# An MLP down-projection in seven block products: eight of its 22 activations, in seven of eight units of a two-layer trunk

## The chip, the cores and the metric

The kernel is one program on one core of a Trainium2 chip. The metric is the device time of one execution in microseconds (us); the kernel before takes 1237.61 us, the median of three runs (1237.38 to 1237.62). A profile comes from one execution of its own.

The engines named here are TensorE (PE; its weight loads are shown as PEld), VectorE (DVE), ScalarE (ACT), GpSimd (POOL) and SyncE (SP), which here issues the DMA transfers of the weights. Each engine works through its own queue of instructions in order, and waits for others by semaphores.

## What is computed

Two layers of a decoder trunk on 512 tokens of 1024 features, in fp32. Each layer is a token mixer (layer 0 attention and short convolution, layer 1 gated linear attention), an MLP, and a gated embedding; all add to the residual `x`. The change is in the second matrix product of the MLP, with `w_down` of 2816 x 1024:

```python
def _conv_ffn(h, w_up, conv_w, conv_b, w_down):
    u = _causal_depthwise_conv(h @ w_up, conv_w) + conv_b
    gate, up = jnp.split(u, 2, axis=-1)
    return (jax.nn.gelu(gate, approximate=False) * up) @ w_down
...
    x = x + _conv_ffn(_rms_norm(x, ffn_norm[i]), ffn_w_up[i], ffn_conv_w[i], ffn_conv_b[i], ffn_w_down[i])
    x = x + _per_layer_embedding(x, p[i], ple_norm[i], ple_w_gate[i], ple_w_proj[i])
```

## The kernel before

**Layout.** Features lie on the 128 partitions and the 512 tokens along the free axis, so `x` is eight tiles `xT[0..7]` of 128 x 512, and the MLP's 2816 inner features are 22 tiles, the activations f = 0 to 21 (`acts`). A product for eight output features' tiles m = 0 to 7 takes weights of 128 x 128 as the stationary operand and an activation tile as the moving one, and adds up in a PSUM bank of 128 x 512.

**Precision.** Each fp32 operand is cut into a high part of reduced precision (`F32R`) and a low part, the remainder. ScalarE copies the high part, VectorE subtracts it from the source for the low one. `mm3` (L158 to L160) then does three matmuls: high x high, high x low, low x high. For weights the cut is in `cut` (L138 high, L139 low): pieces of 1024 columns, from a tile `raw` (two buffers, loaded by SyncE) into `wh` and `wl` (three buffers each). For activations it is `split` (L102, L103; with a gain L105, L106).

**Down-projection.** `project` runs over four units of two output tiles (256 columns of `w_down`). A unit takes the 22 activations in three chunks of eight, eight and six, each with a load and two cuts (halves by columns, `by="b"`); unit 0 begins with the activations 8 to 15, the others with 0 to 7. So a unit is 22 x 2 x 3 = 132 matmuls of 512 columns, and a layer 528. At a unit's end `done` adds both banks to `xT` (L379 in layer 0, L1056 in layer 1) and prepares the tile for the next norm: `advance` in layer 0 splits it with a gain (L105, L106), squares it (L270) and adds the square to `acc` (L271); `blocks` in layer 1 does the like for block forms. Behind the down-projection L324 sums `acc` over the partitions, and the gated embedding follows (`ple1` in layer 1).

**Activations.** `kept` tiles hold the activations in fp32 as the up-projection makes them. `split_acts` cuts f = 0 to 19 for the down-projection, some by pairs (`split_pair`); the last pair, `y`, is cut by `split_pair(NF - 2, y)` just ahead of it.

**Block products.** The up-projection already uses, for the gate columns of units d = 4 to 10, a scheme in which a product of two matrices, each seen as 2 x 2 blocks, needs seven products of blocks instead of eight. The blocks of the weights are (even or odd feature tile) x (left or right 128 columns), those of the activations (even or odd tile) x (left or right 256 tokens). `seven_forms` makes the weights' sums: a plain cut, then four subtractions (L823, L824, L826, L828) in place, and cuts `t13` (L811, L812, wide) and `t2` (narrow); `seven` does the products with 256 columns each (`product`, L846 to L848), on four token-side sums s1 to s4 (`forms`). It adds up in four places, W, V (banks `pa`), X and Y (banks `ps`), with ScalarE copies that seed one from another (L857, L858, L865, L869), and yields between its parts so that other matmuls can be put there. V belongs to both halves of Y; in the up-projection it is copied to SBUF first (`more`, L862).

**Order.** Most of the queues' order is a scheduler's; `manual_schedule` takes the program's order for the engines that it names, `high_priority` puts instructions ahead. In the up-projection the PE order is the program's. The loads stand on SyncE's queue in order of their issue, and each waits for its `raw` buffer.

Of the kernel before, what the change touches and what calls it, by code (L numbers as in the profile page):

```python
# [9 lines left out]
F32 = mybir.dt.float32  # L10
F32R = mybir.dt.float32r
# [3 lines left out]
ALU = mybir.AluOpType  # L15
# [3 lines left out]
P = 128  # L19
S = 512  # L20
D = 1024
NT = S // P
ND = D // P
DFF = 2816
NF = DFF // P
# [3 lines left out]
ET = mybir.EngineType  # L29
# [28 lines left out]
class Kernel:  # L58
# [92 lines left out]

        return get

    def mm3(self, out, lt, rt, start, stop):

        mm = self.nc.tensor.matmul
        (lh, ll), (rh, rl) = lt, rt
        mm(out, lh, rh, start=start, stop=False)  # L158
        mm(out, lh, rl, start=False, stop=False)  # L159
        mm(out, ll, rh, start=False, stop=stop)  # L160

    def rsqrt(self, out, src, scale):

# [631 lines left out]
                out.append((hl[0][:, c], hl[1][:, c]))  # L795
        return out

    def blocks_of(self, raw):

        rv = raw.rearrange("p (j u) n -> p j u n", u=2)  # L800
        return [[rv[:, :, u, c * P : (c + 1) * P] for c in range(2)] for u in range(2)]

    def cut_blocks(self, src, wide=True):

# [9 lines left out]
        n = 2 if wide else 1  # L814
        return lambda j, c: (h[:, n * j + c, :], l[:, n * j + c, :])

    def seven_forms(self, raw):

        nc = self.nc
        (b11, b12), (b21, b22) = self.blocks_of(raw)  # L820
        plain = self.cut_blocks(raw[:, :, :P])

        nc.vector.tensor_tensor(b11, b12, b11, ALU.subtract)  # L823
        nc.vector.tensor_tensor(b12, b22, b12, ALU.subtract)  # L824
        t13 = self.cut_blocks(raw.rearrange("p (j u) n -> p j u n", u=2)[:, :, 0])
        nc.vector.tensor_tensor(b11, b22, b11, ALU.subtract)  # L826
        t2 = self.cut_blocks(b11, False)
        nc.vector.tensor_tensor(b21, b21, b11, ALU.subtract)  # L828
        return plain, t13, t2

    def seven(self, raw, ws, xg, forms):

        nc = self.nc
        H = S // 2
        mm = nc.tensor.matmul
        W, V = self.pa(), self.pa()[:, :H]
        X, Y = self.ps(), self.ps()
        plain, t13, t2 = ws  # L840

        def product(out, w, c, x, first=False):
            kw = dict(skip_group_check=True)
            for j in range(ND // 2):
                (wh, wl), (xh, xl) = w(j, c), x(j)
                mm(out, wh, xh, start=first and j == 0, stop=False, **kw)  # L846
                mm(out, wh, xl, start=False, stop=False, **kw)  # L847
                mm(out, wl, xh, start=False, stop=j == ND // 2 - 1, **kw)  # L848

        def tokens(u, half):  # L850
            c = slice(half * H, (half + 1) * H)
            return lambda j: (xg[2 * j + u][0][:, c], xg[2 * j + u][1][:, c])

        s1, s2, s3, s4 = (lambda j, q=q: forms[j][q] for q in range(4))
        left, right = slice(0, H), slice(H, S)
        product(W[:, left], plain, 0, tokens(0, 0), True)
        nc.scalar.copy(X[:, left], W[:, left])  # L857
        nc.scalar.copy(Y[:, left], W[:, left])  # L858
        yield
        product(V, t13, 0, s1, True)  # L860
        more = self.sp.tile([P, S], F32, tag="acc", name=self.nm("more"), bufs=1)[:, :H]
        nc.scalar.copy(more, V)  # L862
        product(X[:, left], plain, 1, tokens(1, 0))
        product(Y[:, left], t2, 0, s2)
        nc.scalar.copy(X[:, right], Y[:, left])  # L865
        yield
        last = self.cut_blocks(raw.rearrange("p (j u) n -> p j u n", u=2)[:, :, 1])
        product(X[:, right], t13, 1, s3)
        nc.scalar.copy(Y[:, right], X[:, right])  # L869
        yield  # L870
        product(Y[:, left], last, 1, s4)
        product(X[:, right], last, 0, tokens(1, 1))
        yield X, Y, more

    def ffn(self, i, next_gain):
        nc, a, tc = self.nc, self.a, self.tc
        xg, R = self.xg, None
        gain = self.g_ffn[i]
        wu = a["ffn_w_up"][i].rearrange("(k p) n -> p k n", p=P)
        w0, w1, w2, bb = self.fcv  # L880
        with tc.tile_pool(name=f"ffn{i}", bufs=1) as fp:
# [35 lines left out]
            def column(raw, c):  # L917
                return self.cut(raw[:, :, c * P : (c + 1) * P], "b")
# [21 lines left out]
            def split_acts():  # L940
                for f in (8, 10, 12):
                    split_pair(f)
                split_kept(0)
                split_pair(14)
                split_kept(1)
                for f in (16, 18):
                    split_pair(f)

            def gates(d):
                return slice(256 * d, 256 * d + 256)  # L950
# [16 lines left out]
            def prepare(d):  # L967

                rg, rv = loaded(d)
                w1 = column(rv, 1)  # L970
                ws = self.seven_forms(rg)
                return self.seven(rg, ws, xg, forms), w1, column(rv, 0)

            def begin(d, steps, w):

# [6 lines left out]
            first, last = SEVEN  # L982
            scratch = [self.four(fp, F32) for _ in range(ND // 2)]
            late = None
            for d in range(NF // 2):
                g, y = both(), both()
                if first <= d < last:
                    with tc.manual_schedule(engines={ET.PE}):
# [18 lines left out]
                else:  # L1007
# [4 lines left out]
                    todo = []  # L1012
# [21 lines left out]
                u = place(d)  # L1034
                if u is None:
                    u = y
                nc.vector.tensor_tensor(u, g, y, ALU.mult)
                for j in {0: (0, 1), 1: (2, 3)}.get(d, ()):
                    forms.append(self.sums(j, gain, R, scratch[j]))
            split_pair(NF - 2, y)  # L1040
            self.begin_norm(("a0", "a1"))
            done = self.residual(next_gain)
            if i == 1:
                self.forms = []
                halves = []

                def half():
                    if not halves:
                        x = both()
                        halves.extend([x[:, 0], x[:, 1]])  # L1050
                    return halves.pop(0)

                self.half = half

                def done(m, ps):
                    nc.vector.tensor_tensor(self.xT[m], self.xT[m], ps, ALU.add)  # L1056
                    self.blocks(m, next_gain, half)

            self.project(self.rows(a["ffn_w_down"][i]), acts, ND, done, first=(8,))
            if i == 0:  # L1060
                self.end_norm()
            else:
                self.ple1(fp)

    def p_halves(self, i):
        src = self.a["p"][i, 0].rearrange("(t p) e -> p t e", p=P)
# [700 lines left out]
```

## Time and profile before

| | |
|---|---|
| median of three runs | 1237.61 us |
| the profiled execution | 1237.57 us |
| its span, first to last instruction | 1235.8 us |
| instructions | 16256 |
| TensorE matmuls | 6488 |
| DMA, bytes moved | 117.52 MB, mean 95 GB/s |

How to read the profile: a group's row gives line, engine, operation, output <- inputs, their shapes and how often it occurs; then its busy time in us, the mean of one in ns, and the idle time of the engine just before, with what ended it. A timeline's row gives start and duration in us, and in brackets the idle time before it and its releaser. A stretch's row gives its length, and for each engine the busy time with the number of instructions, then the granted clock of TensorE (1.00 is full speed), the busy share of the DMA engines and GB/s. Matmuls overlap in the pipeline, so their starts tell their rate, not their durations.

### The profile page before, as it was taken

How to read it: one execution, taken by the hardware profiler on the slowest of the kernel's cores; microseconds unless marked ns; L12 is line 12 of the kernel's file. 1: busy time of each engine (PE TensorE's matmuls, PEld its weight loads, DVE VectorE, ACT ScalarE, POOL GpSimd, SP SyncE). 2: the span in 40 equal slices, each digit the busy share in tenths (PEclk: the TensorE clock that was granted, in tenths of full speed). 3: DMA queues.
4: the chain of work that ended last, by engine and by line, in shares of the span. 5: the costliest groups of instructions: out<-in, count | busy, mean ns of one | idle time of the engine just before them, and what ended most of it. 6: DMA issues, size and time to landing. Idle time of an engine off the chain costs nothing.

```text
span 1235.8 us, 16256 instructions
## 1 busy us (share of the span) xinstructions
PE 1225.1 (99%) x6488; PEld 1037.8 (84%) x6488; DVE 857.8 (69%) x1337; ACT 611.8 (50%) x975; POOL 44.2 (4%) x64
## 2 busy tenths in 40 slices
PE   9999999999999999999999999999999999999998
PEld 8877788889899888888987888888889989888887
DVE  6886556987778933346679875549977779744495
ACT  7466343555556732234563554435455556533374
POOL 3500000000000000000100000000000000000000
PEclk9999999999999999999999999999999999999999
DMA  7321232323232322222322222332332323322411
GB/s 216 95 79 54 87 103 69 102 69 126 80 112 94 128 94 94 94 85 93 111 91 68 70 68 69 103 99 81 101 109 72 127 79 111 119 94 94 154 42 69
DMA packets 111008, 117.52 MB, mean 95 GB/s; under 512 B 2728, under 2 KB 106210, under 8 KB 110932
## 3 DMA queue, kind: packets, MB, share of 16 engines
q1 hardware_dynamic: 109568, 115.35, 28.4%
q8 instruction: 51, 0.84, 0.3%
q0 software_dynamic: 560, 0.42, 0.3%
q10 hardware_dynamic: 804, 0.70, 0.2%
q14 instruction: 25, 0.20, 0.0%
HBM read 114.37 MB, written 2.10 MB: 94 GB/s over the span
## 4 chain that ended last, share of the span: by engine, by line
PE 88%; DVE 7%; ACT 2%; issue 2%; POOL 1%; DMA 0%; SPq 0%; DVEq 0%; ACTq 0%; POOLq 0%
PE ps L158 18%; PE ps L159 18%; PE ps L160 18%; PE pa L159 5%; PE pa L158 5%; PE pa L160 5%; PE ps L848 3%; PE ps L847 3%; PE ps L846 3%; DVE wl L139 1%; PE pa L848 1%; PE pa L847 1%; PE pa L846 1%; PE ps L1181 1%; PE ps L1179 1%
## 5 line engine op out<-in xcount | busy, mean ns | idle before, releaser
L138 ACT ACTIVATE wh<-raw 128x1024 fp32r<-128x1024 f32 (+4 forms) x184 | 184.3, 1003 | 312.3 <-PE ps L159 258.5
L139 DVE TENSOR_TENSOR wl<-raw,wh 128x1024 fp32r<-128x1024 f32 (+4 forms) x184 | 212.0, 1153 | 166.3 <-ACT wh L138 165.9
L158 PE MATMUL ps<-a,wh 128*128 128x512 f32 x416 | 162.7, 391 | 0.0
L159 PE MATMUL ps<-a,wh 128*128 128x512 f32 x416 | 162.3, 390 | 0.0
L160 PE MATMUL ps<-a,wl 128*128 128x512 f32 x416 | 162.0, 390 | 0.0
L158 PE MATMUL ps<-b,wh 128*128 128x512 f32 x320 | 126.0, 395 | 0.5 <-ACT b L102 0.5
L160 PE MATMUL ps<-b,wl 128*128 128x512 f32 x320 | 125.7, 393 | 0.0
L159 PE MATMUL ps<-b,wh 128*128 128x512 f32 x320 | 125.0, 391 | 0.0
L158 PEld LDWEIGHTS ps<-a,wh 128*128 128x128 f32 x416 | 78.1, 188 | 16.6 <-issue 0.7
L159 PEld LDWEIGHTS ps<-a,wh 128*128 128x128 f32 x416 | 78.2, 188 | 16.3 <-issue 0.3
L160 PEld LDWEIGHTS ps<-a,wl 128*128 128x128 f32 x416 | 78.1, 188 | 16.2
L158 PE MATMUL pa<-a,wh 128*128 128x512 f32 x224 | 87.8, 392 | 0.0
L159 PE MATMUL pa<-a,wh 128*128 128x512 f32 x224 | 87.8, 392 | 0.0
L158 PE MATMUL ps<-four,wh 128*128 128x512 f32 x224 | 87.2, 389 | 0.0
L159 PE MATMUL ps<-four,wh 128*128 128x512 f32 x224 | 87.2, 389 | 0.0
L160 PE MATMUL pa<-a,wl 128*128 128x512 f32 x224 | 87.1, 389 | 0.0
L160 PE MATMUL ps<-four,wl 128*128 128x512 f32 x224 | 87.1, 389 | 0.0
L158 PEld LDWEIGHTS ps<-b,wh 128*128 128x128 f32 x320 | 60.0, 188 | 14.0 <-ACT b L102 1.3
L900 DVE SCALAR_TENSOR_TENSOR zt<-z,vfa,zt 128x511 f32<-128x511 f32 (+1 forms) x92 | 66.9, 744 | 5.9 <-ACT zt L898 5.4
L160 PEld LDWEIGHTS ps<-b,wl 128*128 128x128 f32 x320 | 60.1, 188 | 12.6
L159 PEld LDWEIGHTS ps<-b,wh 128*128 128x128 f32 x320 | 60.1, 188 | 12.4
L811 ACT ACTIVATE wh<-raw 128x1024 fp32r<-128x1024 f32 x42 | 44.4, 1057 | 41.1 <-DVE raw L824 22.1
(423 smaller groups left out, 2620.9 us busy)
## 6 DMA issues: line engine op xcount, KB each, us to landing
raw<-in_ffn_w_up_dram SPq DMA_DIRECT2D x44, 1024.0 KB, 5.0
raw<-in_ffn_w_down_dram SPq DMA_DIRECT2D x16, 1024.0 KB, 4.7
raw<-in_hy_w_in_dram SPq DMA_DIRECT2D x8, 1024.0 KB, 5.1
raw<-in_gla_w_in_dram SPq DMA_DIRECT2D x8, 1024.0 KB, 5.4
raw<-in_ffn_w_down_dram SPq DMA_DIRECT2D x8, 768.0 KB, 4.1
raw<-in_ple_w_gate_dram SPq DMA_DIRECT2D x6, 1024.0 KB, 4.8
raw<-in_gla_w_out_dram SPq DMA_DIRECT2D x4, 1024.0 KB, 4.7
raw<-in_gla_w_in_dram SPq DMA_DIRECT2D x4, 672.0 KB, 4.0
```

Source lines behind the costliest of these rows:

```text
L138: nc.scalar.activation(hv, v, AF.Copy)
L139: nc.vector.tensor_tensor(lv, v, hv.bitcast(F32), ALU.subtract)
L158: mm(out, lh, rh, start=start, stop=False)
L159: mm(out, lh, rl, start=False, stop=False)
L160: mm(out, ll, rh, start=False, stop=stop)
L811: nc.scalar.activation(h, src, AF.Copy)
L846: mm(out, wh, xh, start=first and j == 0, stop=False, **kw)
L847: mm(out, wh, xl, start=False, stop=False, **kw)
L848: mm(out, wl, xh, start=False, stop=j == ND // 2 - 1, **kw)
L900: nc.vector.scalar_tensor_tensor(out=y[:, tap:], in0=z[:, : S - tap], scalar=w[:, f : f + 1], in1=y[:, tap:], op0=ALU.mult, op1=ALU.add,)
L1179: mm(o, lh, rh, start=first and j == 0, stop=False, **kw)
L1181: mm(o, ll, rh, start=False, stop=j == J - 1, **kw)
```

## The change

The 22 rows of activations become A (8 to 13), B (0 to 7) and C (14 to 21). `project` is replaced, for this product alone, by `down`. A unit's C part is done by `seven` in units 0 to 3 of layer 0 and 0 to 2 of layer 1; A and B, and C in unit 3 of layer 1, stay direct. The direct work is a written list `plan` of steps (unit, rows, first and last tile within them, and the unit whose blocks are interleaved, if any), each of three or four tiles and one cut by rows (`by="a"`). In a blocked step, two direct tiles' runs of six matmuls alternate with the parts of `seven`: six direct, W (12), six direct, V with X left and Y left (36), six direct, X right (12), six direct, Y left and X right (24). `pump` counts the three `wh`/`wl` pairs and lets out the next cuts as pairs come free: a cut takes one, a unit's `prepare` two.

V stays in PSUM, and is added from there to both halves of `xT[2s+1]` (L1237); X and Y are added to `xT` as well as the direct banks are (L1170). In layer 0, unit 3 continues its direct sums in X and Y. The C parts of unit 1, and in layer 0 of unit 3, are loaded into the two `zt` tiles, by parity of the row tile, rather than into `raw`. `finish`, which is `advance` or `blocks`, runs for a unit once all blocked steps are done and its sums are complete.

The activations 14 to 21 are cut after the plan's steps 0 to 3 by `split_blocks`, which also makes the token-side sums, two subtractions and additions per half tile, and cuts them into `a0`, `a1`. In the whole program PE has 252 matmuls more: 84 of 256 columns for 48 of 512, seven times. The diff follows, without the three lines in which `mm3` hands on keyword arguments and those in which the up-projection calls the changed functions.

```diff
--- before.py
+++ after.py
@@ -795,10 +795,10 @@
                 out.append((hl[0][:, c], hl[1][:, c]))
         return out
 
-    def blocks_of(self, raw):
+    def by_parity(self, raw):
 
         rv = raw.rearrange("p (j u) n -> p j u n", u=2)
-        return [[rv[:, :, u, c * P : (c + 1) * P] for c in range(2)] for u in range(2)]
+        return rv[:, :, 0], rv[:, :, 1]
 
     def cut_blocks(self, src, wide=True):
 
@@ -814,21 +814,29 @@
         n = 2 if wide else 1
         return lambda j, c: (h[:, n * j + c, :], l[:, n * j + c, :])
 
-    def seven_forms(self, raw):
+    def seven_forms(self, ev, od, raw=None):
 
         nc = self.nc
-        (b11, b12), (b21, b22) = self.blocks_of(raw)
-        plain = self.cut_blocks(raw[:, :, :P])
+        b11, b12, b21, b22 = ev[:, :, :P], ev[:, :, P:], od[:, :, :P], od[:, :, P:]
+        if raw is not None:
+            plain = self.cut_blocks(raw[:, :, :P])
+        else:
+            h, l = (self.wp.tile([P, 1024], F32R, tag=g, name=self.nm(g), bufs=3) for g in ("wh", "wl"))
+            h, l = (x.rearrange("p (j u n) -> p j u n", u=2, n=P) for x in (h, l))
+            for u, b in enumerate((b11, b21)):
+                self.split((h[:, :, u], l[:, :, u]), b)
+            plain = lambda j, c: (h[:, j, c], l[:, j, c])
 
         nc.vector.tensor_tensor(b11, b12, b11, ALU.subtract)
         nc.vector.tensor_tensor(b12, b22, b12, ALU.subtract)
-        t13 = self.cut_blocks(raw.rearrange("p (j u) n -> p j u n", u=2)[:, :, 0])
+        t13 = self.cut_blocks(ev)
         nc.vector.tensor_tensor(b11, b22, b11, ALU.subtract)
         t2 = self.cut_blocks(b11, False)
         nc.vector.tensor_tensor(b21, b21, b11, ALU.subtract)
         return plain, t13, t2
 
-    def seven(self, raw, ws, xg, forms):
+    def seven(self, od, ws, xg, forms, keep=True):
 
 
 
@@ -858,13 +866,15 @@
         nc.scalar.copy(Y[:, left], W[:, left])
         yield
         product(V, t13, 0, s1, True)
-        more = self.sp.tile([P, S], F32, tag="acc", name=self.nm("more"), bufs=1)[:, :H]
-        nc.scalar.copy(more, V)
+        more = V
+        if keep:
+            more = self.sp.tile([P, S], F32, tag="acc", name=self.nm("more"), bufs=1)[:, :H]
+            nc.scalar.copy(more, V)
         product(X[:, left], plain, 1, tokens(1, 0))
         product(Y[:, left], t2, 0, s2)
         nc.scalar.copy(X[:, right], Y[:, left])
         yield
-        last = self.cut_blocks(raw.rearrange("p (j u) n -> p j u n", u=2)[:, :, 1])
+        last = self.cut_blocks(od)
         product(X[:, right], t13, 1, s3)
         nc.scalar.copy(Y[:, right], X[:, right])
         yield
@@ -941,10 +951,28 @@
                 for f in (8, 10, 12):
                     split_pair(f)
                 split_kept(0)
-                split_pair(14)
                 split_kept(1)
-                for f in (16, 18):
-                    split_pair(f)
+            down_forms = []
+            def split_blocks(f, x=None):
+                if x is None:
+                    x = kept[f // 4][:, f % 4 : f % 4 + 2]
+                split_pair(f, x)
+                H = S // 2
+                e, o = x[:, 0], x[:, 1]
+                nc.vector.tensor_tensor(o[:, H:], e[:, H:], o[:, H:], ALU.add)
+                nc.vector.tensor_tensor(e[:, H:], e[:, :H], e[:, H:], ALU.subtract)
+                nc.vector.tensor_tensor(e[:, :H], o[:, H:], e[:, :H], ALU.subtract)
+                nc.vector.tensor_tensor(o[:, :H], o[:, :H], e[:, :H], ALU.subtract)
+                (s2, s3), (s4, s1) = map(split_halves, (e, o))
+                down_forms.append((s1, s2, s3, s4))
+            def split_halves(x):
+                h, l = self.pair(self.fp, "a0", "a1")
+                self.split((h, l), x)
+                return [(h[:, c], l[:, c]) for c in (slice(0, S // 2), slice(S // 2, S))]
 
             def gates(d):
                 return slice(256 * d, 256 * d + 256)
...
@@ -1037,9 +1066,8 @@
                 nc.vector.tensor_tensor(u, g, y, ALU.mult)
                 for j in {0: (0, 1), 1: (2, 3)}.get(d, ()):
                     forms.append(self.sums(j, gain, R, scratch[j]))
-            split_pair(NF - 2, y)
             self.begin_norm(("a0", "a1"))
-            done = self.residual(next_gain)
+            finish = lambda m: self.advance(m, next_gain)
             if i == 1:
                 self.forms = []
                 halves = []
@@ -1051,16 +1079,165 @@
                     return halves.pop(0)
 
                 self.half = half
-
-                def done(m, ps):
-                    nc.vector.tensor_tensor(self.xT[m], self.xT[m], ps, ALU.add)
-                    self.blocks(m, next_gain, half)
-
-            self.project(self.rows(a["ffn_w_down"][i]), acts, ND, done, first=(8,))
+                finish = lambda m: self.blocks(m, next_gain, half)
+            work = [lambda f=f, x=x: split_blocks(f, x) for f, x in ((14, None), (16, None), (18, None), (20, y))]
+            self.down(i, acts, down_forms, both, work, finish)
             if i == 0:
                 self.end_norm()
             else:
                 self.ple1(fp)
+    def down(self, i, acts, forms, both, work, finish):
+        nc, tc = self.nc, self.tc
+        H = S // 2
+        wd = self.a["ffn_w_down"][i].rearrange("(k p) n -> p k n", p=P)
+        rows = {"A": (8, 14), "B": (0, 8), "C": (14, 22)}
+        plan = [(0, "A", 0, 3), (0, "A", 3, 6), (0, "B", 0, 4), (0, "B", 4, 8)]
+        plan += [(1, "A", 0, 3), (1, "A", 3, 6), (1, "B", 0, 4), (1, "B", 4, 8, 0)]
+        plan += [(2, "B", 0, 4, 1), (2, "B", 4, 8, 2)]
+        if i == 0:
+            plan += [(2, "A", 0, 4, 3), (2, "A", 4, 6), (3, "B", 0, 4), (3, "B", 4, 8), (3, "A", 0, 3), (3, "A", 3, 6)]
+            loads = ["A0", "B0", "A1", "B1", "C0", "B2", "C2", "A2", "B3", "A3"]
+            inner = ["C1", "C3"]
+        else:
+            plan += [(2, "A", 0, 3), (2, "A", 3, 6), (3, "B", 0, 4), (3, "B", 4, 8)]
+            plan += [(3, "C", 0, 4), (3, "C", 4, 8), (3, "A", 0, 3), (3, "A", 3, 6)]
+            loads = ["A0", "B0", "A1", "B1", "C0", "B2", "C2", "A2", "B3", "C3", "A3"]
+            inner = ["C1"]
+        blocked = 4 - i
+        plan = [p if len(p) == 5 else p + (None,) for p in plan]
+        got, cuts, gens = {}, {}, {}
+        def cols(u):
+            return slice(2 * P * u, 2 * P * u + 2 * P)
+        def load(key):
+            k0, k1 = rows[key[0]]
+            u = int(key[1])
+            raw = self.raw(k1 - k0, 2 * P)
+            nc.sync.dma_start(raw, wd[:, k0:k1, cols(u)])
+            got[key] = (raw, None)
+        def load_inner(key):
+            k0, k1 = rows[key[0]]
+            u = int(key[1])
+            parts = []
+            for q in range(2):
+                t = both().rearrange("p a (b n) -> p (a b) n", n=2 * P)
+                nc.sync.dma_start(t, wd[:, k0 + q : k1 : 2, cols(u)])
+                parts.append(t)
+            got[key] = (None, parts)
+        def cut(t):
+            u, name, k0, k1, _ = plan[t]
+            cuts[t] = self.cut(got[f"{name}{u}"][0][:, k0:k1], "a")
+            if k1 == rows[name][1] - rows[name][0] and loads:
+                load(loads.pop(0))
+        def prepare(u):
+            raw, parts = got[f"C{u}"]
+            ev, od = parts or self.by_parity(raw)
+            ws = self.seven_forms(ev, od, raw)
+            gens[u] = self.seven(od, ws, acts[14:], forms, False)
+        def cut_done(u):
+            raw, _ = got[f"C{u}"]
+            if raw is not None and loads:
+                load(loads.pop(0))
+            elif raw is None and inner:
+                load_inner(inner.pop(0))
+        todo = []
+        for t, p in enumerate(plan):
+            todo.append((1, lambda t=t: cut(t)))
+            if p[4] is not None:
+                todo.append((2, lambda u=p[4]: prepare(u)))
+        free = 3
+        def pump(n):
+            nonlocal free
+            free += n
+            while todo and todo[0][0] <= free:
+                need, f = todo.pop(0)
+                free -= need
+                f()
+        def add(m, ps):
+            nc.vector.tensor_tensor(self.xT[m], self.xT[m], ps, ALU.add)
+        due = [2 if u < blocked else 1 for u in range(4)]
+        block_left = blocked
+        next_unit = 0
+        banks = {}
+        with tc.manual_schedule(engines={ET.PE}):
+            with tc.high_priority(offset=300):
+                for _ in range(2):
+                    load(loads.pop(0))
+                pump(0)
+            for t, (u, name, k0, k1, s) in enumerate(plan):
+                own = u not in banks
+                if own:
+                    banks[u] = [self.ps(), self.ps()]
+                ends = t + 1 == len(plan) or plan[t + 1][0] != u
+                joined = i == 0 and u == 3
+                def steps(lo, hi):
+                    for k in range(lo, hi):
+                        for c in range(2):
+                            self.mm3(
+                                banks[u][c], cuts[t](k, c * P, (c + 1) * P), acts[rows[name][0] + k0 + k],
+                                start=own and k == 0, stop=ends and k == k1 - k0 - 1, skip_group_check=joined,
+                            )
+                def settled(ends):
+                    nonlocal next_unit
+                    if ends:
+                        for c in range(2):
+                            add(2 * u + c, banks[u][c])
+                        due[u] -= 1
+                    while not block_left and next_unit < 4 and not due[next_unit]:
+                        for m in (2 * next_unit, 2 * next_unit + 1):
+                            finish(m)
+                        next_unit += 1
+                if s is None:
+                    steps(0, k1 - k0)
+                    settled(ends)
+                    pump(1)
+                    if work:
+                        work.pop(0)()
+                        if not work:
+                            load_inner(inner.pop(0))
+                else:
+                    g = gens[s]
+                    steps(0, 1)
+                    next(g)
+                    steps(1, 2)
+                    next(g)
+                    steps(2, 3)
+                    next(g)
+                    cut_done(s)
+                    pump(1)
+                    steps(3, 4)
+                    settled(ends)
+                    pump(1)
+                    X, Y, V = next(g)
+                    if i == 0 and s == 3:
+                        banks[3] = [X, Y]
+                    else:
+                        add(2 * s, X)
+                        add(2 * s + 1, Y)
+                    pump(1)
+                    x = self.xT[2 * s + 1].rearrange("p (u t) -> p u t", u=2)
+                    nc.vector.tensor_tensor(x, x, V.unsqueeze(1).to_broadcast([P, 2, H]), ALU.add)
+                    due[s] -= 1
+                    block_left -= 1
+                    settled(False)
 
```

More of the change, by code (lines that the diff above doesn't have):

```diff
@@ L152, in cut, with mm3 @@
         return get
-    def mm3(self, out, lt, rt, start, stop):
+    def mm3(self, out, lt, rt, start, stop, **kw):
         mm = self.nc.tensor.matmul
         (lh, ll), (rh, rl) = lt, rt
-        mm(out, lh, rh, start=start, stop=False)
-        mm(out, lh, rl, start=False, stop=False)
-        mm(out, ll, rh, start=False, stop=stop)
+        mm(out, lh, rh, start=start, stop=False, **kw)
+        mm(out, lh, rl, start=False, stop=False, **kw)
+        mm(out, ll, rh, start=False, stop=stop, **kw)
     def rsqrt(self, out, src, scale):
@@ L970, in prepare @@
                 w1 = column(rv, 1)
-                ws = self.seven_forms(rg)
-                return self.seven(rg, ws, xg, forms), w1, column(rv, 0)
+                ev, od = self.by_parity(rg)
+                ws = self.seven_forms(ev, od, rg)
+                return self.seven(od, ws, xg, forms), w1, column(rv, 0)
             def begin(d, steps, w):
```

## The prediction

> **What bounds the kernel now.** I read first the page's busy times and chain of waits, then a table of the two down-projections by stretch, then groups and single instructions.
>
> ```profile
> span 1235.8 us, 16256 instructions
> PE 1225.1 (99%) x6488; PEld 1037.8 (84%) x6488; DVE 857.8 (69%) x1337; ACT 611.8 (50%) x975; POOL 44.2 (4%) x64
> PE 88%; DVE 7%; ACT 2%; issue 2%; POOL 1%; DMA 0%; SPq 0%; DVEq 0%; ACTq 0%; POOLq 0%
> ```
>
> TensorE is busy 99% of the span and carries 88% of the chain. The time outside the span is 1237.57 - 1235.8 = 1.8 us; the profiled execution lies 0.04 us under the median of the runs, 1237.61, so a sum against the one serves for the other.
>
> The stretches below are: layer 0's down-projection, the 13 us behind it, and the same two of layer 1.
>
> ```profile
> core 0: us, PE busy (x) PEld busy (x) DVE busy (x) ACT busy (x) POOL busy (x), PEclk, DMA share, GB/s
> 419.35:539.05 119.70, 119.70 (x530) 99.11 (x529) 51.61 (x59) 37.90 (x46) 0.00 (x0) 1.00 0.28 92
> 539.05:552.20 13.15, 13.15 (x68) 11.08 (x66) 5.50 (x10) 4.32 (x7) 1.01 (x1) 1.00 0.37 130
> 1056.98:1176.69 119.71, 119.71 (x531) 99.14 (x529) 59.59 (x79) 44.51 (x60) 0.00 (x0) 1.00 0.36 122
> 1176.69:1196.00 19.31, 19.31 (x98) 16.07 (x96) 19.09 (x23) 14.80 (x22) 1.87 (x1) 1.00 0.03 11
> ```
>
> In both down-projections PE is busy all the time, at full clock, while VectorE works 43 to 50% of it and ScalarE 32 to 37%. Each holds 528 matmuls of 512 columns (the counts include two or three neighbours at the edges), so one costs 119.70/528 = 0.2267 us from start to start. Only less PE work, or a new PE wait, can move the time there.
>
> **The matmuls removed and added.** A matmul's own duration overlaps its neighbours', so I price by starts. The rows are the first matmul of successive runs in the up-projection, which already uses the seven-product form.
>
> ```profile
> 298.66 0.40 PE L158 MATMUL pa<-a,wh 128*128 128x512 f32 x1
> ...
> 300.05 0.28 PE L846 MATMUL pa<-b,wh 128*128 128x256 f32 x1
> ...
> 304.35 0.40 PE L158 MATMUL pa<-a,wh 128*128 128x512 f32 x1
> ...
> 307.10 0.28 PE L846 MATMUL ps<-b,wh 128*128 128x256 f32 x1
> ...
> 308.53 0.40 PE L158 MATMUL pa<-a,wh 128*128 128x512 f32 x1
> ```
>
> 36 matmuls of 256 columns took 304.35 - 300.05 = 4.30 us and 12 took 308.53 - 307.10 = 1.43: 0.119 each. Six of 512 between them took 300.05 - 298.66 = 1.39, against 6 x 0.2267 = 1.36. (Means of durations, 0.40 to 0.28, would call 84 against 48 a loss.) In a unit, eight activations by two columns by three is 48 matmuls: 10.88 us. Seven products are 84 half-width matmuls, in runs of 12, 36, 12 and 24: 1.43 + 4.30 + 1.43 + 2.87 = 10.03. Four interleaved short runs cost 0.03 more each, 0.12. Saved: 0.73 per unit, four units in layer 0 and three in layer 1: **-5.1**.
>
> The Trainium skill's page "TensorE: Matmul & The Clock Gate", section "Back-to-back issue gap", speaks against this: the sustained spacing is set by the weight load as well as the matmul, about 81 ns at 128 columns and 131 at 512. An estimate between these, about 98 ns at 256, would make the 84 cost 8.2 us and the 48 only 6.3, a loss of 13 us over seven units. The rows disagree: 119 ns against 227, nearly in proportion to the columns.
>
> **What must keep up.** The added work per blocked unit, from the up-projection's groups:
>
> ```profile
> L139 DVE TENSOR_TENSOR wl<-raw,wh 128x1024 fp32r<-128x1024 f32 x148 | 180.8, 1222 | 113.8 <-ACT wh L138 113.5
> L138 ACT ACTIVATE wh<-raw 128x1024 fp32r<-128x1024 f32 x148 | 156.4, 1059 | 242.1 <-PE ps L159 196.6 <-issue 20.1 <-DMA raw<-in_ffn_w_up_dram 15.8
> L823 DVE TENSOR_TENSOR raw<-raw 128x512 f32<-128x512 f32 x14 | 9.5, 681 | 0.0
> L812 DVE TENSOR_TENSOR t<-raw,t 128x512 fp32r<-128x512 f32 x14 | 9.6, 684 | 0.0
> L379 DVE TENSOR_TENSOR xT<-xT,ps 128x512 f32<-128x512 f32 x24 | 16.5, 687 | 45.9 <-PE ps L160 45.9
> L857 ACT COPY ps<-pa 128x256 f32<-128x256 f32 x14 | 5.0, 357 | 15.7 <-PE pa L848 15.7
> L869 ACT COPY ps<-ps 128x256 f32<-128x256 f32 x14 | 5.0, 360 | 18.1 <-PE ps L848 18.1
> ```
>
> VectorE gets, per blocked unit, four subtractions of 0.68, three wide cuts of 1.22 (before: two), one narrow of 0.68, and three more additions of 0.69: some 7 us. Over the 119.7 - 2.9 us of layer 0 its busy time goes to some 51.6 + 4 x 7 + four `split_blocks` (four half subtractions and two cuts, some 2.8 each) = 91 us, under PE's. A blocked step lasts 15.6 us of PE and carries about 10.5 of VectorE. Throughput is covered; the question is order within a step. Three wh/wl pairs hand out the pace, and consecutive steps follow without a break (plan steps 7, 8, 9 and, in layer 0, 10). Loads are no concern: in these rows one lands in about 5 us,
>
> ```profile
> raw<-in_ffn_w_down_dram SPq DMA_DIRECT2D x16, 1024.0 KB, 4.7
> raw<-in_ffn_w_down_dram SPq DMA_DIRECT2D x8, 768.0 KB, 4.1
> ```
>
> and on SP's queue the tightest, C1 in the two zt tiles, is issued some 17 us before its first use; the others have at least a step.
>
> **The handover from unit 0 to unit 1.** This is where I find a wait. In a queue an instruction follows at less than its own duration:
>
> ```profile
> 413.81 1.06 ACT L138 ACTIVATE wh<-raw 128x1024 fp32r<-128x1024 f32 x1 [0.50 <-PE ps L847]
> 414.77 0.36 ACT L869 COPY ps<-ps 128x256 f32<-128x256 f32 x1
> ...
> 1184.32 2.35 DVE L1168 TENSOR_TENSOR raw<-four,raw 128x1024 f32<-128x1024 f32 x2
> 1186.59 0.15 DVE L167 TENSOR_SCALAR rs<-pa 128x4 f32<-128x4 f32 x1
> 539.25 0.69 DVE L379 TENSOR_TENSOR xT<-xT,ps 128x512 f32<-128x512 f32 x1 [0.73 <-PE ps L160]
> 539.86 0.69 DVE L139 TENSOR_TENSOR wl<-raw,wh 128x512 fp32r<-128x512 f32 x1
> ```
>
> So VectorE: 1.14 for 1024 columns, 0.61 for 512; ScalarE 0.96 for 1024. Put T at the start of the last six 512-matmuls of unit 0's step. PE reaches V of unit 1 after 6, 24, 6, 12 and 6 matmuls: 1.39 + 2.87 + 1.39 + 1.43 + 1.39 = T + 8.5, and needs the low part of `t13` at its third, T + 8.75. In the changed kernel's compiled order VectorE does, from T + 0.9 (first result of unit 1's bank plus the 0.2 between 539.05 and 539.25): addition, wide cut, two additions, half a plain cut (to 4.4), an addition that waits for X's end at T + 4.26 (to 5.1), the other half, L831, V's addition, L832 (to 7.5). `t13`'s high part on ScalarE stands behind the copies of W (L865, L866), and these wait for W's end at T + 7.1, plus 0.23 to see it, two times 0.3: it starts at 7.9, ends at 9.0; the low part ends on VectorE at 10.25. PE is late by 10.25 - 8.75 = 1.5 us, and by some 0.1 more for the restart: **+1.6 in each layer, +3.2**. Bounds: nothing if both queues ran 1.5 us ahead of this; 1.6 as worked. I take 1.6, since three instructions in a row have a named waiter. What is late next is only V's product; the copies and cuts behind it move with it.
>
> At unit 1 to 2, and in layer 0 at 2 to 3, `t13`'s high part stands ahead of the W copies: the same count gives T + 8.4 to 8.5 against 8.75, a cover of 0.25 to 0.4 us. I take nothing; gone, it costs those copies' 0.6 and up to 1.6. The first blocked step has some 2 us of cover by the count from its plan steps.
>
> **The copy L879.** Y right <- X right stands on ScalarE behind a wide high cut (rows 413.81 and 414.77: 0.96). X right's six-matmul cover is 1.39; latency 0.23 plus 0.96 plus 0.36 exceeds it by 0.16 where the cut starts just then. At five of the seven steps (units 0 to 2 of layer 0, 0 and 1 of layer 1), about 0.1 each: **+0.5** (0 to 0.8).
>
> **The seams.**
>
> ```profile
> 541.41 0.69 DVE L271 TENSOR_TENSOR acc<-acc,sq 128x512 f32<-128x512 f32 x1
> ...
> 543.14 0.95 PE L324 MATMUL pa<-ones,acc 128*128 128x1 f32 x8
> ...
> 1196.03 0.19 PEld L159 LDWEIGHTS pa<-wl,four 128*128 128x128 f32 x1 [0.41 <-DVE wl L1159]
> 1196.04 0.50 PE L159 MATMUL pa<-wl,four 128*128 128x512 f32 x1
> ```
>
> The last two columns now end together, so both columns' splits and squares come after. In layer 0 acc was ready at 542.10, 1.04 before L324; the second pair of ScalarE operations brings it to about the same moment: 0 to 0.3. In layer 1 VectorE is full in its 19 us (19.09 of 19.31) and already makes PE wait at 1196; it is put back by about 0.15. Together **+0.2** (0 to 0.5). `split_pair` for 14, 16 and 18 leaves the stage's start and its four-fold larger successor fills idle VectorE time of plan steps 0 to 3; uncovered, one such would cost some 5 us, and none of its results is due before V at step 7.
>
> **Sum.** -5.1 + 3.2 + 0.5 + 0.2 = -1.2: 1237.6 - 1.2 = **1236.4 us**. What a measurement of this kernel can tell from no change is 0.2%, 2.5 us.
>
> **The rivals.** (A) The cover holds everywhere: ScalarE and VectorE run as far ahead as in the up-projection, where PE shows no wait at the same products. For it: that row 300.05 to 304.35 without a gap; against it: there 12 to 24 matmuls of the value product give longer cover. 1237.6 - 5.1 = 1232.5. (B) Slower: VectorE's queue comes late at every handover, because L832 ends later than T + 7.3 there too; that is decided by 0.3 us, a single addition's half. Five handovers (three in layer 0, two in layer 1) at 1.6 = 8.0, and 0.7 for the rest: 1237.6 - 5.1 + 8.7 = 1241.2. For it: the small cover; against: the count. (C) Half-width matmuls are spaced by their weight load, not their columns:
>
> ```profile
> L158 PEld LDWEIGHTS ps<-a,wh 128*128 128x128 f32 x416 | 78.1, 188 | 16.6 <-issue 0.7
> ```
>
> 84 x 0.188 = 15.8 against 10.9, +4.9 in each of seven units: 1272. Against it: the same loads stand behind the 0.119 of the up-projection. By the skill's section named above it would be about 1251. (D) The blocks do not pay as said, because C1 in the zt tiles comes late by a load (5 us each layer): 1236.4 + 10 = 1246; against it the 17 us.
>
> **The numbers.** Forecast 0.52, A 0.25, B 0.17, C 0.01, D 0.02, and 0.03 for what I have not named. The forecast's own range, with the bounds of its terms, is 1234.8 to 1238.2; reaching to A and B gives 1232.6 to 1241.2. Faster by over 0.2% means under 1235.1: A and a tenth of the forecast's cases, 0.30. Slower means over 1240.1: B's most, C, D, 0.20. The same: 0.50.
>
> **What would show it.** Right: 6740 PE matmuls (252 more); runs of 12 and 36 half-width matmuls at 0.119; one PE wait of about 1.5 us per layer, on V of unit 1, ended by DVE wl L812; small waits on X or Y after L879; none at the value of L324 over 0.3. Wrong: waits of over a microsecond at unit 2 or 3, at the plain cut of C1 (DMA), or in plan steps 0 to 6, which I count as free.

## The result and the profile after

The changed kernel takes 1242.45 us, the median of six runs (1240.41 to 1243.64), against 1237.61 (1237.21 to 1238.42). The ratio is 1.0036, 95% interval 1.0023 to 1.0049: slower by 0.36%, where 0.1% faster was forecast, and 1.2 us above the end of the range, 1241.2. Two runs, at 1240.41 and 1240.73, had a mean granted clock of 1.000; the other four, 1242.04 to 1243.64, had 0.997 or 0.998. The profiled execution is one of the four, 1243.01 us.

First the page of the kernel after: its span, the engines, the clock in 40 slices, and the chain of waits.

```profile
span 1241.2 us, 16978 instructions
PE 1225.9 (99%) x6740; PEld 1047.2 (84%) x6740; DVE 920.4 (74%) x1449; ACT 640.2 (52%) x1036; POOL 42.7 (3%) x64
PEclk9999999999999999999999999999999999999989
PE 87%; DVE 8%; ACT 3%; issue 2%; POOL 1%; ACTq 0%; DVEq 0%; POOLq 0%
```

The shares look as before. What differs is one digit of the clock, in the last slice but one, and the waits. Here are TensorE's waits of both kernels (line and what it waited for, us in total, times, longest), without those of the start: first before, then after.

```profile
PE pa L1447 <- DVE F L1445: 1.5, 2, 1.0
```

```profile
PE ps L1357 <- DVE wl L1336: 2.2, 1, 2.2
PE pa L856 <- DVE wl L812: 1.5, 2, 0.8
PE pa L1624 <- DVE F L1622: 1.5, 2, 1.0
...
PE pa L854 <- ACT wh L811: 0.7, 2, 0.4
```

L1447 before is L1624 after. New are L854 and L856, at V of unit 1, once in each layer, and one wait of 2.2 us at L1357. That line is not in the down-projection: it is in the gated embedding behind it, in layer 1's seam (the passage from the one to the other).

To see where the 5.4 us between the two profiled executions (1243.01 against 1237.57) came from, I took the same points in both traces. The windows of the kernel after are layer 0's down-projection, layer 1's, and from the end of this to the last matmul; below them is the last of these before.

```profile
419.02:538.21 119.19, 118.07 (x675) 103.10 (x674) 83.73 (x116) 53.44 (x79) 0.00 (x0) 1.00 0.30 94
1056.70:1176.37 119.67, 118.55 (x638) 102.04 (x637) 87.92 (x128) 56.45 (x84) 0.00 (x0) 1.00 0.38 126
1176.37:1236.48 60.11, 57.92 (x277) 48.72 (x275) 42.90 (x55) 33.55 (x51) 1.01 (x1) 0.94 0.08 31
```

```profile
1176.69:1231.33 54.64, 54.64 (x277) 46.01 (x275) 42.20 (x52) 33.02 (x48) 1.87 (x1) 1.00 0.10 38
```

The two stages came out at 119.19 and 119.67 us against 119.70 and 119.71: -0.51 and -0.04. The stretch behind layer 1 has the same 277 matmuls and went from 54.64 to 60.11: **+5.47, the whole loss**. (The rest is +0.5 over code that is the same in both, and the ends of the span.)

What happened there stands on the timelines of the kernel after, first VectorE's, then ScalarE's and TensorE's, start and duration in us.

```profile
1175.89 1.36 DVE L1170 TENSOR_TENSOR xT<-xT,ps 128x512 f32<-128x512 f32 x2
1177.17 1.22 DVE L1336 TENSOR_TENSOR four<-raw,four 128x1024 fp32r<-128x1024 f32 x1
1178.41 0.43 DVE L103 TENSOR_TENSOR b<-zt,b 128x256 fp32r<-128x256 f32 x1
1178.75 0.69 DVE L280 TENSOR_TENSOR acc<-acc,sq 128x512 f32<-128x512 f32 x1
...
1181.30 0.69 DVE L280 TENSOR_TENSOR acc<-acc,sq 128x512 f32<-128x512 f32 x1
1181.90 1.29 DVE L103 TENSOR_TENSOR b<-zt,b 128x512 fp32r<-128x512 f32 x2
1183.11 1.23 DVE L1336 TENSOR_TENSOR wl<-raw,wh 128x1024 fp32r<-128x1024 f32 x1
```

```profile
1179.94 1.04 ACT L1335 ACTIVATE wh<-raw 128x1024 fp32r<-128x1024 f32 x1
```

```profile
1181.81 0.39 PE L1356 MATMUL ps<-wh,a 128*128 128x512 f32 x1
1184.39 0.50 PE L1357 MATMUL ps<-wl,a 128*128 128x512 f32 x1 [2.19 <-DVE wl L1336]
...
1190.92 0.63 PE L1357 MATMUL ps<-wl,a 128*128 128x512 f32 x1
1191.35 0.63 PE L1358 MATMUL ps<-wh,a 128*128 128x512 f32 x1
```

And this is VectorE's timeline of the kernel before (L1056 is the addition, L1159 the low cut):

```profile
1173.51 0.68 DVE L1056 TENSOR_TENSOR xT<-xT,ps 128x512 f32<-128x512 f32 x1
...
1176.89 0.69 DVE L1056 TENSOR_TENSOR xT<-xT,ps 128x512 f32<-128x512 f32 x1 [0.28 <-PE ps L160]
...
1180.51 1.22 DVE L1159 TENSOR_TENSOR wl<-raw,wh 128x1024 fp32r<-128x1024 f32 x1
1181.64 0.68 DVE L103 TENSOR_TENSOR b<-zt,b 128x512 fp32r<-128x512 f32 x1
1182.24 0.41 DVE L308 TENSOR_TENSOR zt<-zt,zt 128x256 f32<-128x256 f32 x1
...
1183.71 0.68 DVE L103 TENSOR_TENSOR b<-zt,b 128x512 fp32r<-128x512 f32 x1
```

After the change both columns' additions come at 1175.89, one behind the other, since both banks end together. VectorE then does all the block forms of both, and the low cut that TensorE needs at 1182.04 stands last, at 1183.11, though its high part had been ready since 1180.98. Before, column 6's addition was at 1173.51, and this cut stood ahead of three of the forms and was through at 1181.73.

Behind the wait the next matmul starts after 0.33 us instead of 0.23, a restart that costs 0.10; from some 0.9 us behind the wait's end on, matmuls of 512 columns follow at 0.43 us. The windows, with the granted clock in the third place from the end, show the wait, the five matmuls behind it, and two stretches after:

```profile
1181.80:1184.39 2.59, 0.40 (x3) 0.01 (x1) 2.56 (x5) 0.25 (x1) 0.00 (x0) 1.00 0.00 0
1184.39:1185.50 1.11, 1.11 (x5) 0.87 (x6) 1.11 (x1) 0.00 (x0) 0.00 (x0) 0.92 0.00 0
1185.50:1192.00 6.50, 6.50 (x25) 5.82 (x24) 3.69 (x6) 3.95 (x6) 1.01 (x1) 0.50 0.00 0
1192.00:1198.00 6.00, 6.00 (x30) 4.92 (x30) 5.03 (x7) 3.66 (x5) 0.00 (x0) 0.99 0.00 0
```

So there are two losses in the seam of this execution: some 2.5 us of wait and restart, and then half clock, some 3 us. In windows of 0.1 us the half clock lasts from 1185.3 to 1192.2, 6.8 us. By their mean clocks, four runs of six had the second loss.

### The profile page after: what moved, and what is told of

It reads as the page before. It is cut to its first block, busy times and chain, and to the rows that moved or that the text cites. A ratio compares the mean times of both kernels' runs of the same rounds, so it can differ in the third digit from the quotient of the medians.

```text
span 1241.2 us, 16978 instructions
## 1 busy us (share of the span) xinstructions
PE 1225.9 (99%) x6740; PEld 1047.2 (84%) x6740; DVE 920.4 (74%) x1449; ACT 640.2 (52%) x1036; POOL 42.7 (3%) x64
## 4 chain that ended last, share of the span: by engine, by line
PE 87%; DVE 8%; ACT 3%; issue 2%; POOL 1%; ACTq 0%; DVEq 0%; POOLq 0%
PE ps L158 16%; PE ps L159 16%; PE ps L160 16%; PE pa L159 5%; PE pa L158 5%; PE pa L160 5%; PE ps L854 4%; PE ps L856 4%; PE ps L855 4%; PE pa L856 2%; PE pa L855 2%; PE pa L854 2%; DVE wl L139 1%; PE ps L1357 1%; PE ps L1358 1%
## 5 line engine op out<-in xcount | busy, mean ns | idle before, releaser
L138 ACT ACTIVATE wh<-raw 128x1024 fp32r<-128x1024 f32 (+4 forms) x170 | 169.3, 998 | 225.4 <-PE ps L159 167.9
L139 DVE TENSOR_TENSOR wl<-raw,wh 128x1024 fp32r<-128x1024 f32 (+4 forms) x170 | 194.9, 1147 | 94.6 <-ACT wh L138 94.2
L811 ACT ACTIVATE wh<-raw 128x1024 fp32r<-128x1024 f32 x54 | 57.1, 1058 | 69.1 <-DVE raw L832 30.1
L812 DVE TENSOR_TENSOR wl<-raw,wh 128x1024 fp32r<-128x1024 f32 x54 | 65.9, 1221 | 28.0 <-ACT wh L811 27.9
L160 PEld LDWEIGHTS pa<-a,wl 128*128 128x128 f32 x224 | 42.1, 188 | 9.2
L158 PEld LDWEIGHTS pa<-a,wh 128*128 128x128 f32 x224 | 42.3, 189 | 7.3
```

The source lines that it names most:

```text
L138: nc.scalar.activation(hv, v, AF.Copy)
L139: nc.vector.tensor_tensor(lv, v, hv.bitcast(F32), ALU.subtract)
L158: mm(out, lh, rh, start=start, stop=False, **kw)
L160: mm(out, ll, rh, start=False, stop=stop, **kw)
L811: nc.scalar.activation(h, src, AF.Copy)
L812: nc.vector.tensor_tensor(l, src, h.bitcast(F32), ALU.subtract)
```

## The experiments

Each is compared with runs of the kernel before on the same chip: 1237.81 (27 runs) for the first four, 1237.72 (16) for the last three. The changed kernel's own 1242.45 stands beside 1237.61, so a difference taken from it directly can be off by some 0.2 us.

**Columns apart.** Column 6's bank ends earlier again, in layer 1 alone.

```diff
-                    for k in range(lo, hi):
-                        for c in range(2):
+                    last = i == 1 and t + 1 == len(plan)
+                    for k, c in sorted(((k, c) for k in range(lo, hi) for c in range(2)), key=lambda x: last * x[1]):
```

> The changed kernel, but the last step of the plan in layer 1 goes column by column, so that the bank of column 6 ends 9 matmuls (2.0 us) before that of column 7. In the compiled order the low cut that TensorE waited 2.2 us for (L1336) moves from the 13th to the 6th place behind column 6's addition. Theory (the wait in the seam of layer 1 comes from both columns ending together, and the half clock behind it from the wait): no PE wait on L1336 over 0.3 us, granted clock 1.00 in every run, and the 5.5 us that the seam lost are back to within 1 us: about 1237.3. Rival (the half clock belongs to the denser half-width matmuls of the stage, not to the wait): only the wait's 2.4 us come back, about 1240, and some runs still show a clock of 0.997.

Measured: 1237.86 us (1237.59 to 1238.39, 11 runs), ratio 1.0000 (0.9991 to 1.0009), and a clock of 0.999 or 1.000 in every run. The wait on L1336 at L1357 is gone. VectorE's timeline in its seam:

```profile
1175.48 0.69 DVE L1170 TENSOR_TENSOR xT<-xT,ps 128x512 f32<-128x512 f32 x1
...
1177.56 0.68 DVE L1170 TENSOR_TENSOR xT<-xT,ps 128x512 f32<-128x512 f32 x1
...
1179.09 1.22 DVE L1336 TENSOR_TENSOR wl<-raw,wh 128x1024 fp32r<-128x1024 f32 x1
...
1184.18 0.68 DVE L103 TENSOR_TENSOR b<-zt,b 128x512 fp32r<-128x512 f32 x1
```

The additions are 2.1 us apart, and the cut runs 4.0 us earlier, ahead of most of the forms, though this stage began 1.0 us later (1057.68 against 1056.70). Of the 4.84 us that the median had lost to the kernel before, 0.05 is left, and in the trace the stretch behind layer 1 takes 54.54 us, against 60.11 in the changed kernel and 54.64 before. The theory holds, and the half clock went with the wait, though the stage's half-width matmuls were all there.

**Low cut first.** The same cut, by priority alone; both columns still end together.

```diff
-        wt1 = [chunk(b11[:, :2, :])]
+        with tc.high_priority(offset=300): wt1 = [chunk(b11[:, :2, :])]
```

> The changed kernel, but with the chunk that TensorE waited for in layer 1's seam (high and low cut of the first half of t1) given priority: on VectorE it follows the two additions and the low cut before it, ahead of all the block forms; both columns still end together. If only the order on VectorE is at fault: no wait there, no half clock, about 1237.3. If the work of column 6, now 2 us later in a stretch where VectorE was busy 19.09 of 19.31 us, is at fault: the wait is put off, in smaller pieces of some 1.5 us in all up to 1196 us, with no half clock: about 1239.

Measured: 1238.48 us (1237.45 to 1238.86, 11 runs), ratio 1.0005 (0.9996 to 1.0013). No wait at L1357, no half clock. A smaller delay of 0.3 us and a restart of 0.1 appeared behind the first matmul of the projection, at 1196.2 us, where in the kernel before they were 0.16 and 0.10. Over the kernel before 0.67 us is left of 4.84, so the place in the queue accounts for some 4.2 us, and column 6's later work for at most the 0.6 us by which this run lies above the one before, less than the 1.5 us that I had allowed it.

**Blocks first.** Against the wait at V of unit 1.

```diff
-            ws = self.seven_forms(ev, od, raw)
+            with tc.high_priority(offset=300): ws = self.seven_forms(ev, od, raw)
```

(in `prepare` of `down` alone)

> The changed kernel, but the weights' block forms of the next unit have priority over the additions to the residual in the down-projection. In the compiled order at unit 0 to 1 the high part of t13 then stands ahead of the two copies of W, and X's and V's additions behind L832. By the count t13's low part ends at T + 8.1 instead of T + 10.25, before the 8.75 at which TensorE needs it. Theory: no PE wait on the cuts of L811 and L812 in the stage (before: 0.53 + 0.92 and two restarts of 0.10 in each layer), 3.3 us less in all, about 1239.2 with the seam of layer 1 as it is. Rival: the wait moves to X or Y through the later additions, and the time stays within 1 us of the changed kernel's 1242.4.

Measured: 1238.50 us (1237.32 to 1239.76, 11 runs), ratio 1.0004 (0.9995 to 1.0013). ScalarE's and VectorE's timelines at V of unit 1 in layer 0:

```profile
469.44 1.06 ACT L811 ACTIVATE wh<-zt 128x1024 fp32r<-128x1024 f32 x1 [3.27 <-DVE zt L832]
470.40 0.61 ACT L267 ACTIVATE acc<-xT 128x512 f32<-128x512 f32 x1
471.21 0.36 ACT L865 COPY ps<-pa 128x256 f32<-128x256 f32 x1 [0.20 <-PE pa L856]
```

```profile
470.53 1.23 DVE L812 TENSOR_TENSOR wl<-zt,wh 128x1024 fp32r<-128x1024 f32 x1
```

The high part now stands ahead of the copies of W, and the low part is there at 471.76. The waits on L811 and L812 are gone in both layers; the seam's wait of 2.2 us stayed. Since the median mixes clocks, I compare like with like: the five runs at 1.000 took 1237.32 to 1237.68, against 1240.41 and 1240.73 of the changed kernel, so 3.1 us less, near the 3.3 expected; in the traces the two stages together are 3.1 us shorter as well. In place of the wait came a restart of 0.09 us in each layer, at the first matmul into unit 2's second bank, whose weight load waits for a later addition (L1170).

**Y copy on VectorE.** Against the waits on L879.

```diff
-        nc.scalar.copy(Y[:, right], X[:, right])
+        (nc.scalar.copy if keep else nc.vector.tensor_copy)(Y[:, right], X[:, right])
```

> The changed kernel, but the copy of X right into Y right (L879) in the down-projection is done by VectorE, not ScalarE, where it stood behind a wide cut of 0.96 us. Theory: the five waits on it (0.13 and a restart of 0.10, each) go, 1.0 us less in all: about 1241.4. Rival: VectorE is behind at these moments too, and the waits stay or grow: 1242.4 or more.

Measured: 1242.35 us (1242.16 to 1242.39, 5 runs), ratio 1.0036 (1.0023 to 1.0050). The five waits are gone in the trace; 0.05 and a restart of 0.10 came in layer 0's unit 3, which had not waited. The median is the rival's number, and in the time the gain is not shown: all five runs were at a clock of 0.996 or 0.997, and the changed kernel's own runs at 0.997 lie between 1242.87 and 1243.64. So it is the trace that shows the gain: layer 0 takes 122.64 us from its first matmul to L324, against 123.26 in the changed kernel, and layer 1's down-projection 119.14 against 119.67, 1.15 us less in all.

**All three together.**

> The changed kernel with all three edits at once: the last step of layer 1 column by column, the next unit's block forms ahead of the additions, and the copy L879 on VectorE. If the waits are all that stood between the changed kernel and the saving of its matmuls, the gains add: 1237.86 (columns apart) less 3.3 (the waits at V) less 0.9 (the copies): about 1233.7, a ratio to the kernel before of 0.9966, with no PE wait over 0.3 us in either down-projection. If the mended waits only give way to other ones: 1235.5 or more.

Measured: 1233.90 us (1233.57 to 1234.09, 6 runs), ratio 0.9969 (0.9957 to 0.9981). The gains add; this version beats the kernel before by 0.31%. From each stage's first matmul to the first L324 behind it, layer 0 takes 121.39 us and layer 1 124.67, against 123.79 and 126.51 before: -2.40 and -1.84. With the waits that are left, 0.33 in each layer and 0.16 in layer 0, the saving of the matmuls themselves is 2.9 (2.40 + 0.33 + 0.16) and 2.2 (1.84 + 0.33), the 0.73 for each unit that I had worked out.

**Wait filled.** Nine matmuls on constants are added ahead of the product that waits; they are in no result.

```diff
-            add(None, "s1", wt1, first=True, order=steps[:2])
+            _ = [nc.tensor.matmul(Q[0], self.ones_r, self.ones_r.unsqueeze(1).to_broadcast([P, NT, P]), start=True, stop=True) for _ in range(9)]; add(None, "s1", wt1, first=True, order=steps[:2])
```

> The changed kernel with nine matmuls of 512 columns on constants (9 x 0.227 = 2.0 us, into a bank that is begun anew right after) ahead of the block product whose second matmul waits for L1336 in the seam of layer 1; they add to no result. TensorE stays busy through most of the 2.2 us and still waits for the same cut until the same moment. Theory (the half clock follows from the idle time): granted clock 1.00 in every run and all runs at about 1240.5, the time of the changed kernel's two runs at full clock. Rival (it follows from the load of the stage before): more matmuls change nothing or make it worse: 1242 to 1243 and clocks of 0.997 in most runs.

Measured: 1240.05 us (1239.66 to 1240.77, 11 runs), ratio 1.0020 (1.0011 to 1.0029), and a clock of 0.999 or 1.000 in every run. The windows are the filled wait, what follows, and the stretch that was at half clock:

```profile
1182.30:1184.86 2.56, 2.42 (x11) 1.68 (x9) 2.53 (x5) 0.23 (x1) 0.00 (x0) 1.00 0.00 0
1184.86:1187.75 2.89, 2.89 (x21) 2.67 (x22) 2.41 (x3) 0.65 (x2) 0.33 (x1) 1.00 0.00 0
1187.75:1192.00 4.25, 4.25 (x22) 3.52 (x21) 2.83 (x3) 3.83 (x6) 0.67 (x1) 1.00 0.00 0
```

More matmuls, less time: TensorE was kept busy in the same 2.6 us, and the half clock did not come in any of 11 runs. So the half clock follows from the idle time, not from the load of the stage before.

**Before, with a late cut.** The kernel before, with half cuts repeated so that TensorE waits in the same place.

```diff
-            nc.vector.tensor_tensor(l, src, h.bitcast(F32), ALU.subtract)
+            for o, s, g in [(l, src, h)] + [(l[:, q % 2], src[:, q % 2], h[:, q % 2]) for q in range(3 if count[0] == 3 else 0)]: nc.vector.tensor_tensor(o, s, g.bitcast(F32), ALU.subtract)
```

> The kernel before, with the half cuts of the third chunk in layer 1's gated embedding subtracted three times more (the same values again), so that TensorE waits for it in the seam though nothing of the down-projection is changed; by the compiled order the cut ends at about 1185.0 us instead of 1181.7, against a need at 1182.35: a wait of some 2.6 us. VectorE has no slack there, so 2.2 to 2.9 us are lost by themselves: 1240.0 to 1240.7. Theory (an idle TensorE of over 2 us is enough for the half clock): a half clock of some us behind the wait in most runs, clock 0.996 to 0.998, up to 2.5 us more: 1240.5 to 1243. Rival (it needs the seven products): clock 0.999 to 1.000 in every run.

Measured: 1242.17 us (1240.98 to 1243.07, 5 runs), ratio 1.0034 (1.0021 to 1.0046). Two runs, 1240.98 and 1241.16, were at a clock of 1.000, three, 1242.17 to 1243.07, at 0.997 or 0.998. The two without the half clock lie 0.3 to 0.5 us above the 1240.0 to 1240.7 that I had expected of the wait by itself. The wait, and its windows:

```profile
1184.80 0.50 PE L1180 MATMUL ps<-wl,a 128*128 128x512 f32 x1 [2.61 <-DVE wl L1159]
```

```profile
1182.20:1184.80 2.60, 0.00 (x0) 0.00 (x1) 2.60 (x6) 0.63 (x1) 0.00 (x0) 1.00 0.00 0
1184.80:1186.00 1.20, 1.20 (x5) 0.98 (x6) 1.20 (x2) 0.00 (x0) 0.00 (x0) 0.85 0.00 0
1186.00:1192.30 6.30, 6.30 (x25) 5.62 (x24) 4.40 (x5) 3.95 (x6) 1.01 (x1) 0.50 0.00 0
```

The kernel before, with no half-width matmul in its down-projections, shows the same loss by the same steps, at a late low cut alone.

## Why the prediction was wrong

- **The matmuls**, -5.1: right to the tenth, as all three edits together show (2.9 + 2.2). The rival of the weight load falls.
- **The handover from unit 0 to 1**, +1.6 in each layer: right in place, order and size. These are the changed kernel's timelines in layer 0:

```profile
470.10 0.69 DVE L832 TENSOR_TENSOR zt<-zt,zt 128x512 f32<-128x512 f32 x1
...
472.21 1.23 DVE L812 TENSOR_TENSOR wl<-zt,wh 128x1024 fp32r<-128x1024 f32 x1 [1.42 <-ACT wh L811]
```

```profile
470.57 0.36 ACT L865 COPY ps<-pa 128x256 f32<-128x256 f32 x1 [1.52 <-PE pa L856]
470.84 0.36 ACT L866 COPY ps<-pa 128x256 f32<-128x256 f32 x1
471.10 1.07 ACT L811 ACTIVATE wh<-zt 128x1024 fp32r<-128x1024 f32 x1
```

```profile
472.23 0.39 PE L854 MATMUL pa<-a,wh 128*128 128x256 f32 x1 [0.36 <-ACT wh L811]
472.45 0.28 PE L855 MATMUL pa<-a,wh 128*128 128x256 f32 x1
473.49 0.38 PE L856 MATMUL pa<-a,wl 128*128 128x256 f32 x1 [0.75 <-DVE wl L812]
```

  The high part stands behind the copies, which wait for W. TensorE's starts slip 0.53, 0.10, 0.92 and 0.10 against the cadence: 1.65. The other handovers had no wait, so the rival with a wait at every one falls, though its time was the nearest.
- **The copy L879**, +0.5: right in kind and in number, five; too small by more than half. Four cost 0.13 and a restart of 0.10 each, one 0.18, and 0.06 came at a sixth place: 1.2 in all. I had left the restart out here.
- **The seam of layer 0**, 0 to 0.3: nothing; `acc` ended at 542.22 and L324 began at 542.28.
- **The seam of layer 1**, "put back by about 0.15": this is the step that failed. It cost 2.5 us of wait, and with the half clock 5.5. I had counted how much work VectorE gets there, and not gone through its compiled order. The one instruction that mattered had gone from a place ahead of the last three forms to one behind all of them, because both banks end together. Priority alone brought some 4.2 us of 4.8 back, so the order made nearly all of the loss, not the amount. That a wait of 2.2 us can cost twice its length was not in the sum at all, and none of the signs named for being wrong lay in a seam.

With the seam's +5.5 in place of 0.2 and 1.2 for the copies, the sum is 1237.6 - 5.1 + 3.3 + 1.2 + 5.5 = 1242.5. These terms come from the profiled execution, which took 1243.0; the 0.5 that is left lies in code that is the same in both kernels. That the sum meets the median, 1242.45, is luck, since the median lies among runs with and without the half clock.

The forecast's own range, 1234.8 to 1238.2, was not the sum of its terms' bounds either: 0 to 3.2 for the handover, 0 to 0.8 for the copy and 0 to 0.5 for the seams give 1232.5 to 1237.0. The measured time lies outside both.

## What to carry to other kernels

When a change makes two results end together that used to come one after the other, read the queue of the engine that takes them, instruction by instruction, through the stage behind, and look for the one instruction that the busiest engine needs next; the sum of the work says little. Here the scheduler had put it last. When the busiest engine is made to wait, each wait costs its length and 0.1 us of restart, and here, at 2.2 us and more, often a stretch at half clock as well.

## What was not expected of the hardware

An idle TensorE of 2.2 to 2.6 us in the middle of a kernel was followed, 0.1 to 1.7 us after its end, by a stretch at half clock (a granted clock of 0.50), which cost 1 to 3 us. In the four traces that have it, the stretch lasted 6.8 us three times and 3.4 us once (with the block forms first), so one or two times the same length. The mean clocks fit this: 6.8 us at half clock lower a mean over 1240 us by 0.003 and 3.4 us by 0.001, and these runs show 0.996 to 0.998. It did not come every time: in four of six runs of the changed kernel, six of eleven with the block forms first, all five with the copy moved, three of five of the kernel before with a late cut; never in the 39 runs of the four kernels in which the wait was filled or gone. What decides it from run to run is not shown. Waits of 0.4 and 0.8 us at V of unit 1 left the clock at 1.00, and so did one of 1.0 us in each of two places elsewhere (L600, L1624).

The Trainium skill's page "TensorE: Matmul & The Clock Gate", section "HAM oscillation — how this bites in real kernels", puts the rule at no idle gap over about 3.4 us. Here the measurement decides: gaps of 2.2 and 2.6 us were enough in most runs.
